# Differential attention with plain fp32 products: key halves on two row tiles, a lagged pipeline over query tiles, and tied engine orders

## The chip, the cores and the metric

One of the eight cores of a Trainium2 chip runs the whole program. The metric is device time in microseconds; a second measurement of the same kernel on the same chip is shown by its median and its extremes. Engines are named as in the profile: PE (matrix products; PEld loads its weights), DVE, ACT, POOL, and SP, which only issues transfers.

## The reference, cut to what matters

The program is a three-branch mixer run for two layers (gated scans, differential attention, a second scan), then a convolution/LRU layer and a mixture of experts. The change touches the attention branch of both layers: 1024 tokens, 4 heads, two score sets (c = 0, 1) of width 64 per head, values of width 128.

```python
q = rope(q, pos) * (DIFF_HD ** -0.5); k = rope(k, pos)      # (2, b, 4, 1024, 64)
s = jnp.einsum('cbhqd,cbhkd->cbhqk', qblk, k)
p = jax.nn.softmax(s, axis=-1)
w = p[0] - lam * p[1]
o = jnp.einsum('bhqk,bhkv->bhqv', w, v)                      # v: (b, 4, 1024, 128)
o = rms_norm(o, norm_w) * (1.0 - lambda_init)
y = merge_heads(o) * silu(g)
```

All of it is float32.

## The kernel before

Most products are made of parts in the type fp32r: an operand x is kept as a rounded half xh (fp32r) and a rest xl = x - xh, and `mm3` (L370 to L374) sums xh·yh, xh·yl and xl·yh in PSUM. In the attention stage the projections of heads 0 and 1 (dq0, dk0, dv0) run first, in the stage of the scans. `rope` (L901 to L924) and `values` (L926 to L932) turn the PSUM results into halves h and lo and store both to DRAM (qd, kd, dvd). Then comes a branch (L616), which all engines pass. Behind it the attention stage begins: head 0 runs while the projections of heads 2 and 3 (dq1, dk1, dv1: 24 steps of 24 matmuls) are mixed in, eight steps per query tile (`Q_PER_TILE`); heads 1 to 3 follow.

A head has eight query tiles of 128 rows. For each tile and each c, `scores` makes pS (128x1024, two PSUM banks) from the query halves, stacked on the 128 rows, against the rounded keys (KH, L989) and their rests (KL, L990): four matmuls of 512 columns. DVE takes the row maximum (L992), ACT the exponential with its row sum (L994). One tile later `combine` forms e0 + e1·sm (L1010), transposes it in eight blocks on PE (pW, L1019), evicts them as halves wTh and wTl (ACT and DVE; one in part by POOL, L1029 to L1031), and for every second tile runs 24 matmuls of 256 columns into pO (`mm3`). For every fourth tile pO is squared, summed over features with ones (pN), normed and written to yd. The two weights of the output projection that are not yet in place, and later the others, are loaded in parts (`wo_load`: 256 KB each), rounded by ACT (L1088), and the rest taken by DVE or POOL (L1089).

From head 1 on, the operands lie in ATh and ATl, the buffers of the normalized input, which are free once the projections have read them. Their loads are issued by POOL, one or two per tile, each behind a POOL instruction (`issue_after`, which ties an instruction's place on its engine behind another's without a semaphore).

A scheduler orders the instructions of each engine from program order, priorities and its own costs; each engine then runs in that fixed order. The pools around the change: pS has 2 buffers, tag "t" of `tp` has 3 (shared by pW, pN and the products of the mixed-in projections), pO has 1.

Of the kernel before, what the change touches and what calls it, by code (L numbers as in the profile page):

```python
# [31 lines left out]
Q_PER_TILE = 8  # L32
PRELOAD = (3, 2, 2)
PER = 2
# [186 lines left out]
def r32(ap):  # L221
    return ap.bitcast(F32)
# [7 lines left out]
def kernel(ctx: ExitStack, tc: tile.TileContext, A: dict, out: bass.AP, upto=99, dbg=None):  # L230
# [42 lines left out]
    qd = dr.tile([4, 2, 64, 2, S], F32, name="qd")  # L273
    kd = dr.tile([4, 2, 64, 2, S], F32, name="kd")
    dvd = dr.tile([4, 128, 2, S], F32, name="dvd")
# [446 lines left out]
    for l in range(DEPTH):  # L722
# [175 lines left out]
        def rope(n, hp, i, w, acc, tr, at, eng=G):  # L898
# [19 lines left out]
            sc = 0.125 if n == 0 else 1.0  # L918
            rope.last = (SC.activation(h, pT, AF.Copy, scale=sc),
                         V.scalar_tensor_tensor(lo, pT, sc, r32(h), op0=OP.mult, op1=OP.subtract))  # L920
            dst = (qd, kd)[n][2 * hp:2 * hp + 2, :, :, :, (i - 1) * 128:(i + 1) * 128]
            for m, t in enumerate((h, lo)):
                for c in range(2):
                    SY.dma_start(dst[:, m, :, c].rearrange("h x t -> x h t"), r32(t)[c * 64:c * 64 + 64])  # L924

        def values(hp, i, w, acc, at):  # L926
            p = tokm(acc[0], w, 256, i, tag=acc[1])
            h, lo = place(at[2], [128, 256], F32R), place(at[3], [128, 256], F32R)
            SC.activation(h, p[:, :256], AF.Copy)
            V.tensor_tensor(lo, p[:, :256], r32(h), op=OP.subtract)  # L930
            for m, t in enumerate((h, lo)):
                SY.dma_start(dvd[2 * hp:2 * hp + 2, :, m, i * 128:i * 128 + 128].rearrange("h p c -> p h c"),  # L932
                             r32(t).rearrange("p (h c) -> p h c", h=2))

        at1 = ((st, "q"), (st, "t2r"), (st, "sgb"), (st, "sgb"))
# [25 lines left out]
        epsm = aw.tile([128, 128], F32, name="epsm", bufs=1)  # L961
        V.memset(epsm, EPS)

        def head_prep(h):

            if h == 0:
                QS, KH, KL, v = (hp_.tile([128, 2, S], F32R, tag=n, name=n) for n in ("QS", "KH", "KL", "v"))
            else:
                a, b = (2, 4) if h == 2 else (6, 0)
                QS, KH, KL, v = ATh[:, a:a + 2], ATl[:, a:a + 2], ATh[:, b:b + 2], ATl[:, b:b + 2]  # L970
            loads = [lambda: G.dma_start(QS, qd[h].rearrange("m x c t -> (m x) c t"))]
            for m, K in enumerate((KH, KL)):
                for d_ in range(2):
                    loads.append(lambda m=m, K=K, d_=d_: G.dma_start(K[d_ * 64:d_ * 64 + 64], kd[h, m]))
            loads.append(lambda: G.dma_start(v, dvd[h]))
            vh, vl = (v[:, m].rearrange("p (k d) -> p k d", k=8) for m in range(2))
            return {"h": h, "ops": (QS, KH, KL, vh, vl), "loads": loads}

        def scores(st, i):

            QS, KH, KL = st["ops"][:3]
            sm = aw.tile([128, 8], F32, tag="sm", name="sm", bufs=3)
            e = []
            for c in range(2):
                p = sc_.tile([128, 2, 512], F32, tag="s", name="pS")
                qq = QS[:, c, i * 128:(i + 1) * 128]
                for kc in range(2):
                    kt = slice(kc * 512, kc * 512 + 512)
                    T.matmul(p[:, kc, :], qq, KH[:, c, kt], start=True, stop=False)  # L989
                    T.matmul(p[:, kc, :], qq, KL[:, c, kt], start=False, stop=True)  # L990
                pf = p.rearrange("p a b -> p (a b)")
                V.tensor_reduce(sm[:, c:c + 1], pf, axis=AX.X, op=OP.max, negate=True)  # L992
                ec = aw.tile([128, S], F32, tag=f"e{c}", name=f"e{c}", bufs=3)
                SC.activation(ec, pf, AF.Exp, bias=sm[:, c:c + 1], accum_out=sm[:, 2 + c:3 + c])  # L994
                e.append(ec)
            return i, e, sm

        def combine(st, i, e, sm):


            qh, qi, qp = i // 4, i % 4, i // 2
            if qi == 0:
                st["dg"] = aw.tile([128, 4, 128], F32, tag="dg", name="dg", bufs=1)
                st["pO"] = op_.tile([128, 512], F32, tag="o", name="pO")
            if i % 2 == 0:
                st["w"] = []
            V.reciprocal(sm[:, 4:5], sm[:, 3:4])
            V.tensor_scalar(st["dg"][:, qi], ident, sm[:, 2:3], sm[:, 2:3], op0=OP.mult, op1=OP.mult)
            V.scalar_tensor_tensor(sm[:, 5:6], sm[:, 4:5], nlam[:, l:l + 1], sm[:, 2:3], op0=OP.mult, op1=OP.mult)
            V.scalar_tensor_tensor(e[0], e[1], sm[:, 5:6], e[0], op0=OP.mult, op1=OP.add)  # L1010
            for g in range(2):
                if i % 2 == 0:
                    st["w"].append((aw.tile([128, 4, 256], F32R, tag="wTh", name="wTh", bufs=2),
                                    aw.tile([128, 4, 256], F32R, tag="wTl", name="wTl", bufs=2)))
                wTh, wTl = st["w"][g]
                p = tp.tile([128, 4, 128], F32, tag="t", name="pW")
                for j in range(4):
                    kt = g * 4 + j
                    T.transpose(p[:, j, :], e[0][:, kt * 128:(kt + 1) * 128], ident)  # L1019
                sl = (slice(None), slice(None), slice((i % 2) * 128, (i % 2) * 128 + 128))  # L1020
                if g == 0:
                    SC.activation(wTh[sl], p, AF.Copy)
                    V.tensor_sub(wTl[sl], p, r32(wTh[sl]))
                elif i % 4 == 3:
                    SC.activation(wTh[sl], p, AF.Copy)
                    V.tensor_sub(wTl[sl], p, r32(wTh[sl]))
                else:
                    wf = aw.tile([128, 4, 128], F32, tag="wf", name="wf")
                    SC.activation(wf, p, AF.Copy)  # L1029
                    G.tensor_tensor(wTh[sl], wf, bc(C("ones")[:, None, :], [128, 4, 128]), op=OP.mult)  # L1030
                    st["pool"] = G.tensor_tensor(wTl[sl], wf, r32(wTh[sl]), op=OP.subtract)  # L1031
            if i % 2 == 0:
                return
            vh, vl = st["ops"][3:]
            cs = slice((qp % 2) * 256, (qp % 2) * 256 + 256)
            for kt in range(8):
                wTh, wTl = st["w"][kt // 4]
                mm3(st["pO"][:, cs], vh[:, kt, :], vl[:, kt, :], wTh[:, kt % 4, :], wTl[:, kt % 4, :], kt == 0, kt == 7)
            if qi < 3:
                return  # L1040
            t = slice(qh * 512, qh * 512 + 512)
            f = 2 + st["h"]
            oT = aw.tile([128, 512], F32, tag="oT", name="oT", bufs=1)
            sq = aw.tile([128, 512], F32, tag="sq", name="sq", bufs=1)
            sg = aw.tile([128, 512], F32, tag="sg", name="sg", bufs=1)
            SY.dma_start(sg, sgd[f][:, t])
            SC.activation(oT, st["pO"], AF.Copy)
            SC.activation(sq, st["pO"], AF.Square, scale=128 ** -0.5)
            p = tp.tile([128, 512], F32, tag="t", name="pN")
            for n in range(4):  # L1050
                c = slice(n * 128, n * 128 + 128)
                T.matmul(p[:, c], C("ones"), sq[:, c], start=True, stop=False)
                T.matmul(p[:, c], epsm, st["dg"][:, n], start=False, stop=True)
            G.tensor_tensor(oT, oT, sg, op=OP.mult)
            SC.activation(sq, p, AF.Ln)
            SC.activation(sq, sq, AF.Exp, scale=-0.5)
            V.tensor_tensor(oT, oT, sq, op=OP.mult)
            SY.dma_start(yd[:, f, t], oT)

        def other_projections():  # L1060
            got = {0: wq1}
            at2 = ((hp_, "st"), (aw, "sg"), (hp_, "sh"), (hp_, "sh"))

            def step(n, i):
# [6 lines left out]
                if i == 2 and n < 2:  # L1071
                    with tc.issue_after(rope.last[0].ins), tc.issue_after(rope.last[1].ins):
                        got[n + 1] = load_w(wp, wsrc(l, ("dq1", "dk1", "dv1")[n + 1]), 8, 256)
# [5 lines left out]
        def wo_load(cc):  # L1079
# [11 lines left out]

            return [lambda i=i: part(i) for i in range(4)]


        def run(n):
            for _ in range(n):
                if steps:
                    steps.pop(0)()
# [975 lines left out]
```

## Time and profile before

| what | value |
|---|---|
| median of 3 runs | 2968.61 us (2963.6 to 2981.33) |
| profiled execution | 2970.06 us, span 2968.2 us, mean granted clock 0.962 |
| attention stage, layer 0 | about 459 to 749 us of the span |
| attention stage, layer 1 | about 1283 to 1564 us |

Every duration below is from the profiled execution, whose own time is 1.5 us above the median. In its rows "busy" is the union of an engine's instructions; matmuls overlap, so the cost of a matmul in a stream is the distance between two starts and not its own duration. The granted clock is a share of TensorE's full 2.4 GHz; 0.5 stands for 1.2 GHz.

### The profile page before, as it was taken

Reading aid. Unit: us, or ns where it says so; the run is one execution under the profiler, and the core shown is the slowest. Engines: PE = TensorE matmul, PEld = TensorE weight load, DVE = VectorE, ACT = ScalarE, POOL = GpSimd, SP = SyncE. Lnnn points to the kernel's source line nnn. Section 1 sums busy time; section 2 is a strip of 40 time slices with the busy share of each in tenths; the row PEclk is TensorE's granted clock in tenths of the full one; section 3 lists DMA queues with packets and bytes.
Section 4 is the critical chain, followed back from the end, with each engine's and each line's share of the span. In section 5 each row is a group of like instructions: output and inputs, shape, how many; then the busy total and the mean of one; then the engine's idle time right before and its main releaser. Section 6 shows DMA issues by size and latency. Waiting matters only on the chain. (4 is left out here: it accounts for less than half of the span.)

```text
span 2968.2 us, 41594 instructions
## 1 busy us (share of the span) xinstructions
PE 2693.9 (91%) x15942; PEld 2252.8 (76%) x15942; DVE 1956.8 (66%) x2806; ACT 1374.3 (46%) x2174; POOL 829.3 (28%) x612
## 2 busy tenths in 40 slices
PE   7999998978999999989789999788799999899968
PEld 6887888867988878888679887588677767566558
DVE  6766565579457676755894592754676776665667
ACT  5343322456443433323664313633576676555545
POOL 1323232345114231313451332610221121211122
PEclk9999999989999999999999999999899999999989
DMA  4122235543422212445434322043797998879852
GB/s 152 61 77 77 86 110 136 132 131 84 138 92 66 80 61 86 120 130 143 132 84 137 108 84 78 29 172 136 302 360 286 356 349 299 318 250 351 331 212 81
DMA packets 158270, 476.25 MB, mean 160 GB/s; under 512 B 16096, under 2 KB 69408, under 8 KB 128736
## 3 DMA queue, kind: packets, MB, share of 16 engines
q1 hardware_dynamic: 144224, 408.07, 39.2%
q0 software_dynamic: 13824, 65.28, 7.5%
q8 instruction: 132, 2.16, 0.3%
q14 instruction: 90, 0.74, 0.1%
HBM read 384.03 MB, written 89.26 MB: 159 GB/s over the span
## 5 line engine op out<-in xcount | busy, mean ns | idle before, releaser
L1602 DVE TENSOR_TENSOR ews<-raw,ews 128x2048 fp32r<-128x2048 f32 x168 | 387.7, 2314 | 176.7 <-ACT ews L1601 175.6
L372 PE MATMUL pK<-wh,ATh 128*128 128x256 f32 x1280 | 374.2, 293 | 30.2 <-DVEq L616 11.4
L1601 ACT ACTIVATE ews<-raw 128x2048 fp32r<-128x2048 f32 x172 | 327.2, 1912 | 114.5 <-PE h L374 73.6
L373 PE MATMUL pK<-wl,ATh 128*128 128x256 f32 x1280 | 371.2, 291 | 7.1 <-DVE wl L355 7.1
L374 PE MATMUL pK<-wh,ATl 128*128 128x256 f32 x1280 | 367.2, 289 | 1.8 <-POOL ATl L1366 1.8
L372 PE MATMUL pF<-ATh,wh 128*128 128x512 f32 (+1 forms) x800 | 320.8, 402 | 1.6 <-ACT g L1287 0.7
L373 PE MATMUL pF<-ATl,wh 128*128 128x512 f32 (+1 forms) x800 | 319.9, 400 | 0.3 <-DVE ATl L343 0.2
L374 PE MATMUL pF<-ATh,wl 128*128 128x512 f32 (+1 forms) x800 | 318.8, 399 | 0.1
L372 PEld LDWEIGHTS pK<-wh,ATh 128*128 128x128 f32 x1280 | 250.2, 196 | 38.3 <-issue 21.4
L373 PEld LDWEIGHTS pK<-wl,ATh 128*128 128x128 f32 x1280 | 250.4, 196 | 14.2 <-DVE wl L355 8.0
L374 PEld LDWEIGHTS pK<-wh,ATl 128*128 128x128 f32 x1280 | 249.0, 195 | 4.2 <-POOL ATl L1366 2.0
L994 ACT ACTIVATE e<-pS,sm 128x1024 f32<-128x1024 f32 x128 | 142.9, 1117 | 108.4 <-DVE sm L992 108.0
L372 PEld LDWEIGHTS pF<-ATh,wh 128*128 128x128 f32 (+1 forms) x800 | 149.6, 187 | 39.6 <-issue 3.7
L373 PEld LDWEIGHTS pF<-ATl,wh 128*128 128x128 f32 (+1 forms) x800 | 149.5, 187 | 38.5 <-issue 5.7
L374 PEld LDWEIGHTS pF<-ATh,wl 128*128 128x128 f32 (+1 forms) x800 | 149.3, 187 | 36.7 <-issue 4.5
L373 PE MATMUL h<-ews,xh 128*128 128x512 f32 (+1 forms) x416 | 165.9, 399 | 8.8 <-DVE ews L1602 8.8
L1802 POOL DMA_INDIRECT xb<-hfd,tab x38 | 60.7, 1598 | 401.8 <-PE pT L1782 389.3
L372 PE MATMUL h<-ews,xh 128*128 128x512 f32 (+1 forms) x416 | 167.1, 404 | 4.4 <-ACT ews L1601 4.4
L374 PE MATMUL h<-ews,xl 128*128 128x512 f32 (+1 forms) x416 | 165.9, 400 | 0.0
L992 DVE TENSOR_REDUCE sm<-pS 128x1 f32<-128x1024 f32 x128 | 154.2, 1213 | 11.7 <-PE pS L990 11.5
L373 PE MATMUL pK<-wo,ATh 128*128 128x256 f32 x512 | 145.8, 285 | 0.0
L374 PE MATMUL pK<-wo,ATl 128*128 128x256 f32 x512 | 145.6, 285 | 0.0
(495 smaller groups left out, 6905.3 us busy)
## 6 DMA issues: line engine op xcount, KB each, us to landing
raw<-in_w_dram SPq DMA_DIRECT2D x192, 1024.0 KB, 9.0
ws<-in_wp_dram SPq DMA_DIRECT2D x64, 512.0 KB, 4.5
xd<-x SPq DMA_DIRECT2D x24, 512.0 KB, 2.6
x<-xd SPq DMA_DIRECT2D x17, 512.0 KB, 4.6
x<-in_x_dram SPq DMA_DIRECT2D x16, 512.0 KB, 6.5
sgd<-sgb SPq DMA_DIRECT2D x32, 256.0 KB, 2.0
sg<-sgd SPq DMA_DIRECT2D x32, 256.0 KB, 3.0
yd<-oT SPq DMA_DIRECT2D x32, 256.0 KB, 2.0
```

The costliest lines, as they stand in the source:

```text
L372: T.matmul(ps, ah, bh, start=first, stop=False)
L373: T.matmul(ps, ah, bl, start=False, stop=False)
L374: T.matmul(ps, al, bh, start=False, stop=last)
L992: V.tensor_reduce(sm[:, c:c + 1], pf, axis=AX.X, op=OP.max, negate=True)
L994: SC.activation(ec, pf, AF.Exp, bias=sm[:, c:c + 1], accum_out=sm[:, 2 + c:3 + c])
L1601: SC.activation(w[:, 0], s_, AF.Copy)
L1602: eng.tensor_tensor(w[:, 1], s_, r32(w[:, 0]), op=OP.subtract)
L1802: G.indirect_dma_start(out=xb[:n], out_offset=None, in_=hfd, in_offset=bass.IndirectOffsetOnAxis(ap=idx, axis=0))
```

## The change

Halves go from attention: q, k and v are stored and loaded once, as fp32 (half the bytes), and all products of the stage are plain fp32 matmuls. The scores of a tile and a c are two matmuls of 512 columns, one on rows 0 to 63 with the first 512 keys and one on rows 64 to 127 with the last 512; the queries are therefore loaded twice, into both row halves. The transposed weights are evicted once, by ACT alone. The value products of a pair of tiles are eight fp32 matmuls in four parts of two. A step `period` of a pipeline emits scores of tile i, the combination of tile i-1, transposes of tile i-2, value parts of tiles i-3 and i-4, squares of i-5 and the norm of i-6; `put` ties each emitted instruction behind the last one on its engine (PE, DVE, ACT). Six empty periods drain it at the end. dg is formed on POOL and holds the epsilon, and the sum pN is one matmul instead of eight. `wo` parts are rounded by DVE and their rest is taken by POOL, one period after their load is issued. The operand loads go to SP's queue, not tied; `Q_PER_TILE` is 5, `PRELOAD` (5, 2, 2), `PER` 3.

```diff
@@ rope / values (halves gone; one store instead of two)
-            h, lo = place(at[2], [128, 2, 256], F32R), place(at[3], [128, 2, 256], F32R)
-            rope.last = (SC.activation(h, pT, AF.Copy, scale=sc),
-                         V.scalar_tensor_tensor(lo, pT, sc, r32(h), op0=OP.mult, op1=OP.subtract))
+            h = place(at[2], [128, 2, 256], F32)
+            rope.last = SC.activation(h, pT, AF.Copy, scale=0.125 if n == 0 else 1.0)
@@ loads
+                a = 2 if h == 2 else 6
+                Q, K, v = r32(ATh[:, a:a + 2]), r32(ATl[:, a]), r32(ATl[:, a + 1])
...
+            for d_ in range(2):
+                rows = slice(d_ * 64, d_ * 64 + 64)
+                loads.append(lambda rows=rows: SY.dma_start(Q[rows], qd[h]))
+                loads.append(lambda rows=rows, d_=d_: SY.dma_start(K[rows], kd[h, :, :, d_ * 512:d_ * 512 + 512]))
+            loads.append(lambda: SY.dma_start(v, dvd[h]))
@@ scores
+            for kc in range(2):
+                rows = slice(kc * 64, kc * 64 + 64)
+                put("pe", lambda: T.matmul(p[:, kc, :], Q[rows, c, i * 128:(i + 1) * 128], K[rows, c, :],
+                                           start=True, stop=True))
@@ turned, weighted
+                put("pe", lambda: T.transpose(p[:, j, :], e[0][:, kt * 128:(kt + 1) * 128], ident))
+            put("act", lambda: SC.activation(w[:, :, (i % 2) * 128:(i % 2) * 128 + 128], p, AF.Copy))
...
+            for kt in (2 * part, 2 * part + 1):
+                put("pe", lambda: T.matmul(pO[:, cs], v[:, kt, :], w[kt // 4][:, kt % 4, :], start=kt == 0,
+                                           stop=kt == 7))
@@ period
+            if b[5] and b[5]["i"] % 4 == 3:
+                squared(b[5])
             for c in range(2):
+                if now:
+                    scores(now, c)
+                if c == 0 and b[1]:
+                    combine(b[1])
+                if b[2]:
+                    turned(b[2], c)
+                for n in (3, 4):
+                    if b[n] and b[n]["i"] % 2 == 1:
+                        weighted(b[n], (n - 3) * 2 + c)
+                if c == 0 and b[6] and b[6]["i"] % 4 == 3:
+                    summed(b[6])
+            if b[6] and b[6]["i"] % 4 == 3:
+                headnorm(b[6])
@@ wo_load: run() calls split one period after the load's issue
-                SC.activation(wh[:, i * 2:i * 2 + 2], s_, AF.Copy)
-                (V if i % 2 else G).tensor_tensor(wl[:, i * 2:i * 2 + 2], s_, r32(wh[:, i * 2:i * 2 + 2]),
-                                                  op=OP.subtract)
+                def split():
+                    put("dve", lambda: V.tensor_copy(wh[:, i * 2:i * 2 + 2], s_))
+                    G.tensor_tensor(wl[:, i * 2:i * 2 + 2], s_, r32(wh[:, i * 2:i * 2 + 2]), op=OP.subtract)
```

How the change moves instructions, at three places. First PE in heads 1 to 3 of layer 0, about two tiles (pS: scores, pW: transposes, pO: value products, pN: the norm's sum). Before:

```order
L989 MATMUL pS<-ATl,ATh 128x512
L990 MATMUL pS<-ATh 128x512
L1019 MATMUL pW<-ident,e_7442 128x128 x8
L372 MATMUL pO<-wTh,ATl 128x256
L1019 MATMUL pW<-ident,e_7485 128x128 x8
L989 MATMUL pS<-ATl,ATh 128x512
L990 MATMUL pS<-ATh 128x512
```

After:

```order
L995 MATMUL pS<-ATl,ATh 128x512 x2
L1027 MATMUL pW<-ident,e_6655 128x128 x4
L1042 MATMUL pO<-wT,ATl 128x256 x2
L1058 MATMUL pN<-sq,cst 128x512
L995 MATMUL pS<-ATl,ATh 128x512 x2
L1027 MATMUL pW<-ident,e_6655 128x128 x4
L1042 MATMUL pO<-wT,ATl 128x256 x2
L995 MATMUL pS<-ATl,ATh 128x512 x2
L1027 MATMUL pW<-ident,e_6701 128x128 x4
L1042 MATMUL pO<-wT,ATl 128x256 x2
```

Before, the order is loose: scores of two tiles lie together, and the 24 value products of a pair come in one run (one of them waits in front of a later transpose here). Now each half of a period is a pair of score matmuls, four transposes and two value products.

Second DVE in the same stretch, with the row maxima (sm<-pS), the combination (e) and the weights (wo). Before:

```order
L992 TENSOR_REDUCE sm<-pS 128x1
L1010 SCALAR_TENSOR_TENSOR e_7005<-e_7013,sm,e_7005 128x1024
L1057 TENSOR_TENSOR oT<-oT,sq 128x512
L992 TENSOR_REDUCE sm<-pS 128x1
L1089 TENSOR_TENSOR wo<-wos,wo 128x512
L1023 TENSOR_TENSOR wTl<-pW,wTh 128x4x128
L1008 TENSOR_SCALAR dg<-ident,sm 128x128
L992 TENSOR_REDUCE sm<-pS 128x1
```

After:

```order
L998 TENSOR_REDUCE sm<-pS 128x1
L1012 RECIPROCAL sm<-sm 128x1
L1013 SCALAR_TENSOR_TENSOR sm<-sm,nlam 128x1
L1015 SCALAR_TENSOR_TENSOR e_6572<-e_6593,sm,e_6572 128x1024
L998 TENSOR_REDUCE sm<-pS 128x1
L1122 CAST wo<-wos 128x512
L998 TENSOR_REDUCE sm<-pS 128x1
```

The rests wTl and dg are gone from DVE; the rounding of a part of wo (CAST) stands once per period between two row maxima, in 16 of the 32 periods of a layer.

Third the operand loads of heads 1 and 2, before on POOL between its other work, now on SP. After:

```order
L927 DMA dvd<-pl 128x2x128 x7
L976 DMA ATl<-kd 64x2x512
L975 DMA ATh<-qd 64x2048 x3
L927 DMA dvd<-pl 128x2x128
L976 DMA ATl<-kd 64x2x512
L975 DMA ATh<-qd 64x2048
L976 DMA ATl<-kd 64x2x512
L977 DMA ATl<-dvd 128x1024
L976 DMA ATl<-kd 64x2x512
L977 DMA ATl<-dvd 128x1024
```

The ten loads of both heads stand together, around the last store of the mixed-in projections; of the first four, three are head 2's (1.25 MB), before most of head 1's 2 MB.

## Rows read from the trace of the kernel before

**Rows 1.** Windows: length; busy us (count) by engine; clock, DMA share, GB/s.

```profile
459.00:558.00 99.00, 94.40 (x704) 90.54 (x705) 52.58 (x94) 26.27 (x46) 22.75 (x34) 0.96 0.48 123
558.00:749.00 191.00, 153.04 (x903) 129.19 (x902) 163.35 (x219) 118.47 (x216) 99.86 (x77) 0.91 0.45 120
...
1380.00:1564.50 184.50, 151.78 (x911) 128.06 (x910) 162.99 (x219) 118.00 (x216) 99.81 (x77) 0.93 0.46 124
460.00:480.00 20.00, 16.30 (x104) 15.38 (x103) 7.35 (x17) 2.74 (x4) 3.47 (x6) 0.84 0.99 253
680.00:720.00 40.00, 36.50 (x236) 30.64 (x235) 38.54 (x54) 27.33 (x50) 19.37 (x14) 1.00 0.35 91
735.00:740.00 5.00, 2.10 (x16) 1.87 (x17) 4.96 (x8) 4.13 (x8) 4.47 (x4) 1.00 0.13 49
...
745.00:750.00 5.00, 3.15 (x16) 2.93 (x16) 4.76 (x7) 2.18 (x4) 2.65 (x2) 0.75 0.40 114
```

**Rows 2.** Windows of L994 alone: length, ACT busy us (two records each), clock, DMA.

```profile
558.00:749.00 191.00, 65.01 (x108) 0.91 0.45 120
680.00:720.00 40.00, 16.87 (x28) 1.00 0.35 91
```

**Rows 3.** PE groups, 558 to 749 us: busy, mean ns | idle before, releaser.

```profile
L989 PE MATMUL pS<-ATl,ATh 128*128 128x512 f32 x96 | 42.4, 441 | 19.3 <-ACT e L994 19.3
...
L1019 PE MATMUL pW<-ident,e 128*128 128x128 f32 x232 | 32.7, 283 | 5.8 <-DVE e L1010 5.0 <-ACT wf L1029 0.3
...
L373 PE MATMUL pO<-wTl,ATl 128*128 128x256 f32 x91 | 28.4, 313 | 7.8 <-DVE wTl L1023 7.8
```

**Rows 4.** DVE groups, 558 to 749 us.

```profile
L992 DVE TENSOR_REDUCE sm<-pS 128x1 f32<-128x1024 f32 x53 | 63.9, 1212 | 4.0 <-PE pS L990 3.9
L1010 DVE SCALAR_TENSOR_TENSOR e<-e,sm,e 128x1024 f32<-128x1024 f32 x27 | 36.2, 1341 | 0.6
L1023 DVE TENSOR_TENSOR wTl<-pW,wTh 128x512 fp32r<-128x512 f32 x30 | 20.3, 681 | 0.8 <-ACT wTh L1022 0.8
...
L1089 DVE TENSOR_TENSOR wo<-wos,wo 128x512 fp32r<-128x512 f32 x8 | 6.2, 775 | 11.5 <-ACT wo L1088 11.5
```

**Rows 5.** ACT groups, 558 to 749 us.

```profile
L994 ACT ACTIVATE e<-pS,sm 128x1024 f32<-128x1024 f32 x54 | 60.2, 1117 | 35.5 <-DVE sm L992 35.4
...
L1088 ACT ACTIVATE wo<-wos 128x512 fp32r<-128x512 f32 x16 | 9.8, 634 | 21.3 <-DMA wos<-in_wo_dram 21.3
```

**Rows 6.** PE in order of time (start, us): scores and transposes in a stream.

```profile
688.72 0.39 PE L990 MATMUL pS<-ATh 128*128 128x512 f32 x1
688.95 1.04 PE L1019 MATMUL pW<-ident,e 128*128 128x128 f32 x8
```

**Rows 7.** PE in order of time: one fp32 product of 512 columns.

```profile
154.00 1.02 PE L580 MATMUL pN<-sq,cst 128*128 128x512 f32 x2
...
155.09 0.40 PE L372 MATMUL pF<-ATh,wh 128*128 128x512 f32 x1
```

**Rows 8.** PE in order of time: fp32 products on two row tiles (scan stage).

```profile
304.65 0.61 PE L531 MATMUL pU<-gvv,ki 128*128 128x128 f32 x4
305.19 0.37 PE L542 MATMUL pf<-Qd,Kd 32*128 32x128 f32 x1
305.20 0.37 PE L542 MATMUL pb<-Qd,Kd 32*128 32x128 f32 x1
305.40 0.27 PE L542 MATMUL pf<-Qd,Kd 32*128 32x128 f32 x1
...
306.08 0.27 PE L542 MATMUL pb<-Qd,Kd 32*128 32x128 f32 x1
...
306.62 0.40 PE L372 MATMUL pF<-ATh,wh 128*128 128x512 f32 x1
```

**Rows 9.** PE groups, 459 to 558 us, those with waits.

```profile
L372 PE MATMUL pK<-wh,ATh 128*128 128x256 f32 x192 | 56.8, 296 | 5.9 <-DVEq L616 5.9
...
L990 PE MATMUL pS<-KL,QS 128*128 128x512 f32 x24 | 10.1, 430 | 2.7 <-DMA KL<-kd 2.7
```

More of the change, by code (lines that the diff above doesn't have):

```diff
@@ L968, in head_prep @@
             else:
[L969 to L983, printed above, removed]
-            for c in range(2):
[L985 to L1058, printed above, removed]
@@ new lines, in turned @@
+        def turned(q, g):
+            st, i, e = q["st"], q["i"], q["e"]
+            if i % 2 == 0:
+                st["w"] = st.get("w", [])[:2 * g] if g else []
+                st["w"].append(aw.tile([128, 4, 256], F32, tag="wT", name="wT", bufs=4))
+            p = tp.tile([128, 4, 128], F32, tag="t", name="pW")
+            for j in range(4):
+                kt = g * 4 + j
+                put("pe", lambda: T.transpose(p[:, j, :], e[0][:, kt * 128:(kt + 1) * 128], ident))
+            w = st["w"][g]
+            put("act", lambda: SC.activation(w[:, :, (i % 2) * 128:(i % 2) * 128 + 128], p, AF.Copy))
+            q["w"] = st["w"]
@@ new lines, in weighted @@
+        def weighted(q, part):
+            st, qp = q["st"], q["i"] // 2
+            if part == 0:
+                if qp % 2 == 0:
+                    st["pO"] = op_.tile([128, 512], F32, tag="o", name="pO")
+                q["pO"] = st["pO"]
+            pO, v, w = q["pO"], st["ops"][2], q["w"]
+            cs = slice((qp % 2) * 256, (qp % 2) * 256 + 256)
+            for kt in (2 * part, 2 * part + 1):
+                put("pe", lambda: T.matmul(pO[:, cs], v[:, kt, :], w[kt // 4][:, kt % 4, :], start=kt == 0,
+                                           stop=kt == 7))
@@ new lines, in summed, with headnorm @@
+        def summed(q):
+            p = q["pN"] = tp.tile([128, 512], F32, tag="t", name="pN")
+            put("pe", lambda: T.matmul(p, C("ones"), q["sq"], start=True, stop=True))
+        def headnorm(q):
+            sq, oT, qh = q["sq"], q["oT"], q["i"] // 4
+            put("act",
+                lambda: SC.activation(sq, q["pN"], AF.Ln),
+                lambda: SC.activation(sq, sq, AF.Exp, scale=-0.5))
+            G.tensor_tensor(oT, oT, sq, op=OP.mult)
+            SY.dma_start(yd[:, 2 + q["st"]["h"], qh * 512:qh * 512 + 512], oT)
@@ new lines, in period, with back @@
+        def period(now, qs):
+            def back(n):
+                return qs[-1 - n] if len(qs) > n else None
+            qs.append(now)
+            b = [back(n) for n in range(7)]
+            if b[5] and b[5]["i"] % 4 == 3:
+                squared(b[5])
+            for c in range(2):
+                if now:
[11 more added lines that the diff above has]
+                headnorm(b[6])
@@ L1107 @@
         proj = other_projections()
-        late = None
+        qs = []
         for h in range(4):
@@ L1115 @@
             for i in range(8):
-                now = (ops[h],) + scores(ops[h], i)
-                if late:
-                    combine(*late)
-                late = now
+                period({"st": ops[h], "i": i, "e": [],
+                        "sm": aw.tile([128, 8], F32, tag="sm", name="sm", bufs=4)}, qs)
                 if h < 3 and i == PRELOAD[h]:
@@ L1122 @@
                 for load in next_loads(h):
-                    with tc.issue_after(ops[h]["pool"].ins):
-                        load()
+                    load()
                 run(per)
-        combine(*late)
+        tail = turn["act"]
+        for _ in range(6):
+            period(None, qs)
+            run(0)
         p2.close()
```

90 lines of the change are left out of this document (67 added, 23 removed).

## The prediction

> **What bounds the kernel now.** I first cut the span into stages with the windows view, since the shares of the whole span mix stages with different limits. The attention stage of layer 0 has two stretches [rows 1]. In 459 to 558 us the projections of heads 2 and 3 run mixed with five tiles of head 0, and PE is busy 94.4 of 99.0 us: PE bounds it. From 558 to 749 us 27 tiles are left (108 records of L994, two records for each of two exponentials per tile [rows 2]) and PE is busy 153 of 191 us at a mean granted clock of 0.91, so PE doesn't bound this stretch. DVE does, with interruptions: in 680 to 720 us DVE is busy 38.5 of 40 us, and the 28 records of L994 there are 7 tiles, 5.71 us each. At that rate 27 tiles would take 154 us; the other 37 of the 191 us are stalls and the end.
>
> The groups by line then name the waits. PE's largest is 19.3 us in front of a score matmul until an exponential has freed its PSUM buffer; 7.8 us go to the rest wTl, 5.0 to the combination [rows 3]. The exponentials in turn wait 35.4 us for the row maxima, so the ring goes back to DVE. And ACT stands 21.3 us in front of the rounding of a weight part (L1088) until its load has landed [rows 5]; DVE stands 11.5 us for ACT behind that [rows 4]. These are the stalls: a load that is late stops an engine that the scores need. Layer 1 has the same stretch from 1380 to 1564.5 us, 184.5 us [rows 1].
>
> So the question is what the stretch costs when DVE has less to do, the tied order takes the late loads out of the way, and PE pays for fp32.
>
> **The price of an fp32 product.** The sum pN of the scans is an fp32 matmul of 512 columns in a dense stream: it starts at 154.00, the second matmul behind it at 155.09, and one fp32r matmul of 512 columns (0.23, from the distance in [rows 6]) lies between. So it takes 0.86 us, in two records of 0.43 [rows 7]; 256 columns take 0.43, 128 columns 0.107 per record. A transpose takes 0.11: eight span 1.04 us, of which the last's modelled duration is 0.27 [rows 6].
>
> **Scores.** Removed per tile and c: four fp32r matmuls, 4 x 0.23 = 0.93 us. Added: two fp32 matmuls of 512 columns with 64 rows each. No row shows these. Bounds: side by side 0.86, one after the other 1.72. The nearest rows are fp32 products on two row tiles in the scans [rows 8]: pf and pb start 0.01 us apart, again and again, sixteen records (305.19 to 306.08) in eight steps of 0.11. They run side by side from the first record on. But the excursion has a price: the four records of L531 that start at 304.65 are done at 305.08 (4 x 0.107); the second matmul behind it starts at 306.62, so the stream is back at 306.39. That is 1.31 us for 8 x 0.107 = 0.86 us of work: 0.45 us for going into the row tiles and out. I take 0.86 + 0.44 = 1.30 us for a pair, with 0.86 and 2.16 as ends: every half period enters and leaves the row tiles, since transposes of all 128 rows follow.
>
> **Values, transposes, norm.** A pair of tiles takes eight fp32 matmuls of 256 columns, 3.44 us, where 24 fp32r ones took about 24 x 0.12 = 2.9. Transposes stay. pN is one matmul of 0.86 us for four tiles in place of eight of 128 columns (two records each, 1.7 us).
>
> **PE's work in the long stretch.** With the counts of before: 26 tiles' scores (96 records of L989 for heads 1 to 3 are 24 tiles [rows 3], and two of head 0's are left), 52 x 1.30 = 67.6; 232 transposes, 25.1; 15 pairs of values, 51.6; 7 norms, 6.0. Sum 150.3 us, that is 2.60 + 0.86 + 1.72 + 0.22 = 5.40 per tile.
>
> **Is PE the bound then?** DVE per tile: two maxima 2.42, the combination 1.34, a quarter of a product of 128x512 (0.68, as L1023) 0.17, together 3.9 and the small ones; the rests wTl and dg are gone. In the 16 periods with a weight part 0.78 more, 4.7 [rows 4]. ACT: two exponentials of 1.12 and less than 2 us for the rest. Both are under 5.40. The ring also closes in time: a score pair (1.3), its maximum (1.2) and exponential (1.1) are some 4 us with the handovers, and a buffer comes back after one period. So PE should be the bound, at 0.96 or more of the full clock, as it is at 1.00 in 680 to 720 us, where it is busy 91%.
>
> **What PE's work doesn't cover**, 11 us per layer: the end, where the last maximum, exponential, combination, transposes and eviction follow one another (before, PE idled 4.8 us of 735 to 740 and 745 to 750 [rows 1]; I keep 5); head 1's operands, 2; DVE's short lead in the periods with a weight part and the seams of heads, 4. Of head 1: in SP's order 2.75 MB lie up to its last key part, and at 253 GB/s, the rate of 460 to 480 us [rows 1], that is 11 us and a few for landing. The work ahead of its first scores is six half periods, about 16 us: barely hidden. If it weren't, head 1 would wait, and not SP alone; behind those loads only weight parts queue, each a period ahead of its use. POOL loses the evictions and gets dg and all the rests of the weights; nothing on PE waits for these within a period.
>
> So the stretch takes 150.3 + 11 = 161 us: 30 less in layer 0, 23.5 less in layer 1.
>
> **The first stretch.** PE bounds it and its work grows: 12 pairs of scores by 0.37, a pair of values by 0.6, together 5 us. Against that stand the halved bytes: the 2.7 us wait for KL [rows 9] goes with that operand, some 1 us for KH too, and SP, which PE waits for at the branch for 5.9 us, has half the stores to issue; I take 1.5 for that. Net 0 in both layers. Spreading the projections over more tiles (five steps each) moves work, it adds none.
>
> **Sum.** 2970.06 - 53.5 = 2916.6 us for an execution like the profiled one; the median of before is 1.5 us below that, which gives **2915 us**.
>
> **The rivals.**
> 1. *DVE stays the bound*, because the tied order makes it wait its turn: 5.71 per tile instead of 5.40. For it: the weight parts bring DVE to 4.7 and more, and POOL works beside it. Against: 3.9 in the other half of the tiles. 26 x 0.31 = 8 us per layer: 2932.
> 2. *The weight parts stall DVE as they stalled ACT.* The rounding now stands between two maxima, and an unlanded part stops both. For: ACT lost 21.3 us so. Against: each part has a period between issue and use. If all of it returns, 2 x 21.3: 2958.
> 3. *The row tiles overlap by half.* If matmuls start and end strictly in program order and the second's first record can't start before the first's last, a pair takes three records: 0.43 more for 128 pairs, 55 us: 2970. Against it: [rows 8], where pb's first record starts with pf's first. The Trainium skill's page "TensorE: Matmul & The Clock Gate" (Part 3, under "What overlaps and what doesn't") says that matmuls are strictly in order in start and end, without reordering; by a literal reading of that the sum would be this rival's 2970. The rows of this case differ from that reading at 128 columns; none shows 512.
> 4. *Slower: the row tiles don't overlap at 512 columns*, because the two streams share something that short ones don't fill. A pair then costs 2.16 us: 0.86 x 128 = 110 us more, 3025. This decides from 0.42 more per pair (53.5 / 128) for no gain; from 0.65 more the kernel is over 1% slower. For it only that no row has such a length.
>
> That the change doesn't do what it says is excluded by the order of the instructions: pairs of scores stand side by side in each half period.
>
> **How the numbers follow.** Forecast 0.70, rivals 0.12, 0.06, 0.05, 0.07. A measurement here can tell about 1%, 29.7 us, from no change. Faster by that: the forecast and most of rival 1, 0.80. Within: the rest of it, rivals 2 and 3, 0.13. Slower: rival 4, 0.07. The range reaches down to a price of 1.08 for a pair (half of the 0.44 hidden, 28 us less) with 3 instead of 11 us uncovered, 2915 - 28 - 16 = 2871, and up to rival 2: 2870 to 2960; rivals 3 and 4 are left out.
>
> **What the profile after would show.** Right: in the long stretch PE is busy over 92%, a period of 5.3 to 5.6 us, the first records of a score pair starting within 0.02 us of each other, the wait of scores for exponentials under 5 us per layer, ACT no longer waiting for weights. Wrong: a period of 5.7 with DVE over 95% (rival 1); waits of the rounding on DVE for its load (rival 2); a pair of 1.7 (rival 3) or 2.2 us (rival 4). A long wait of a head's first scores for their loads would make the 2 us too small; a lower granted clock in the stretch would raise every term of PE.

## The result, and the profile after

The changed kernel takes **2928.4 us** in the median of four runs (2926.4 to 2938.8), the kernel before 2966.1 us beside it; the ratio is 0.9871 with a 95% interval of 0.9828 to 0.9914. So it is 38 us faster where 53.5 were forecast; 2928 lies inside the range of 2870 to 2960.

The stretches of the stage in the profiled execution after (its own time is 2938.8 us, the slowest of the four; columns as in [rows 1], the engines in the order PE, PEld, DVE, ACT, POOL). The first four lines are the two stretches of each layer, the fifth four periods in the middle, then the first 20 us behind the branch in both layers, then the end:

```profile
454.60:555.00 100.40, 96.65 (x681) 84.00 (x682) 39.97 (x71) 27.27 (x47) 16.34 (x30) 0.94 0.28 71
555.00:729.30 174.30, 159.08 (x750) 90.86 (x748) 121.92 (x166) 108.98 (x196) 61.06 (x57) 0.99 0.37 101
1259.10:1360.00 100.90, 96.47 (x677) 83.73 (x678) 39.98 (x71) 27.48 (x47) 16.13 (x30) 0.93 0.28 70
1360.00:1538.00 178.00, 160.36 (x754) 90.87 (x753) 122.33 (x167) 109.17 (x197) 60.99 (x57) 0.98 0.36 99
617.98:640.69 22.71, 21.21 (x98) 11.36 (x98) 17.75 (x26) 15.04 (x27) 11.11 (x11) 1.00 0.55 145
454.60:475.00 20.40, 17.47 (x80) 13.75 (x81) 4.99 (x11) 2.30 (x4) 0.45 (x1) 0.69 0.45 105
1259.10:1280.00 20.90, 17.29 (x73) 13.02 (x74) 5.17 (x11) 2.41 (x4) 0.45 (x1) 0.67 0.44 103
705.85:735.00 29.15, 22.20 (x118) 18.88 (x117) 11.55 (x18) 14.07 (x25) 5.10 (x4) 0.88 0.39 118
```

In the long stretch PE went from 80% busy at a clock of 0.91 to 91% at 0.99, and DVE from 86% to 70%: the bound has moved to PE. But four periods take 22.71 us, 5.68 per tile and not 5.40, and PE works only 21.21 of them. The groups of PE in 555 to 729 us say why (columns as in [rows 3]):

```profile
L995 PE MATMUL pS<-ATl,ATh 64*128 64x512 f32 x192 | 54.6, 641 | 0.0
L1042 PE MATMUL pO<-wT,ATl 128*128 128x256 f32 x192 | 50.7, 390 | 7.5 <-DVE oT L1052 7.5
L1042 PE MATMUL pO<-wT,v 128*128 128x256 f32 x56 | 14.5, 382 | 1.0 <-DVE oT L1052 1.0
L1058 PE MATMUL pN<-sq,cst 128*128 128x512 f32 x16 | 8.3, 599 | 1.7 <-POOL sq L1054 1.7
L372 PE MATMUL pK<-wo,ATh 128*128 128x256 f32 x12 | 4.0, 331 | 2.5 <-ACT ATh L1188 2.5
```

The scores' 19.3 us of waiting for exponentials [rows 3] are gone, and ACT no longer waits for weight parts. What is new is a wait of the value products for oT, the product of pO with the gate. One such wait in order of time, all engines:

```profile
637.16 0.38 PE L1042 MATMUL pO<-wT,ATl 128*128 128x256 f32 x1
637.47 1.13 PE L995 MATMUL pS<-ATl,ATh 64*128 64x512 f32 x4
637.74 1.11 ACT L1000 ACTIVATE e<-pS,sm 128x1024 f32<-128x1024 f32 x1 [1.08 <-DVE sm L998]
638.53 0.66 PE L1027 MATMUL pW<-ident,e 128*128 128x128 f32 x4
638.84 0.59 ACT L1029 ACTIVATE wT<-pW 128x512 f32<-128x512 f32 x1
639.32 0.60 ACT L1051 ACTIVATE sq<-pO 128x512 f32<-128x512 f32 x1
639.95 0.69 DVE L1052 TENSOR_TENSOR oT<-pO,sg 128x512 f32<-128x512 f32 x1 [1.91 <-ACT sq L1051]
640.69 0.48 PE L1042 MATMUL pO<-wT,ATl 128*128 128x256 f32 x1 [1.50 <-DVE oT L1052]
```

The last value product of a group starts at 637.16. Its square could follow at 637.5, but ACT's tied order has an exponential and an eviction ahead of it, so it starts at 639.32; DVE's product follows only then, and the single pO buffer is free at 640.7. PE, whose tied order lets nothing else go first, stands 1.50 us in every fourth period.

Where the time went, from starts of the same events in both traces (us from PE's first matmul behind the branch; "last maximum" is the start of the last L992 or L998):

| | layer 0 before | after | layer 1 before | after |
|---|---|---|---|---|
| to the last mixed-in projection | 97.0 | 100.7 | 95.7 | 101.6 |
| from there to the last maximum | 179.8 | 149.3 | 173.7 | 151.3 |
| from there to the end of the output projection | 114.5 | 119.9 | 113.5 | 121.1 |

The long stretch up to the last maximum gained 30.5 and 22.4 us. The first stretch gave back 3.7 and 5.9, the end 5.4 and 7.6. Together that is 30.3 us of the 31.2 by which the two profiled executions differ.

The gain of the long stretch is not a faster tile. In the kernel before, behind the last weight part (its rounding starts at 640.7 us in layer 0), four tiles take 22.5 us, and DVE is busy 21.76 of them:

```profile
694.71:717.20 22.49, 20.23 (x129) 16.85 (x128) 21.76 (x32) 15.41 (x28) 10.94 (x7) 1.00 0.08 24
```

That is 5.6 us per tile, no more than the 5.68 after. What went are the stalls among the weight parts: by the starts of the row maxima, the eight tiles of head 1 took 8.0 us each in layer 0 and 7.7 in layer 1 before, 5.7 and 5.9 after. In layer 0 that is 19 us, beside the 21.3 us that ACT stood for weight parts [rows 5].

### The profile page after: what moved, and what is told of

It reads as the page before. It is cut to its first block, busy times and chain, and to the rows that moved or that the text cites. A ratio compares the mean times of both kernels' runs of the same rounds, so it can differ in the third digit from the quotient of the medians.

```text
span 2936.7 us, 39989 instructions
## 1 busy us (share of the span) xinstructions
PE 2705.7 (92%) x15462; PEld 2156.6 (73%) x15462; DVE 1832.6 (62%) x2614; ACT 1351.8 (46%) x2126; POOL 740.5 (25%) x564
## 5 line engine op out<-in xcount | busy, mean ns | idle before, releaser
L373 PE MATMUL pK<-wl,ATh 128*128 128x256 f32 x1280 | 371.9, 291 | 7.3 <-DVE wl L355 7.3
L998 DVE TENSOR_REDUCE sm<-pS 128x1 f32<-128x1024 f32 x128 | 156.2, 1221 | 112.2 <-PE pS L995 112.2
L372 PE MATMUL pK<-wo,ATh 128*128 128x256 f32 x512 | 148.6, 290 | 10.5 <-ACT ATh L1188 10.5
L373 PE MATMUL pK<-wo,ATh 128*128 128x256 f32 x512 | 147.0, 287 | 0.0
```

Of the source, the lines that this page charges most:

```text
L372: T.matmul(ps, ah, bh, start=first, stop=False)
L373: T.matmul(ps, ah, bl, start=False, stop=False)
L998: put("dve", lambda: V.tensor_reduce(sm[:, c:c + 1], pf, axis=AX.X, op=OP.max, negate=True))
```

## The experiments

Each is an edit of the changed kernel. All ratios are to the kernel before, run on the same chip; its medians on the three chips used are 2966.1, 2969.9 and 2969.5 us. A "stage" is the time from PE's first matmul behind the branch to the end of the output projection, from the traces.

**The base once more.**

> The changed kernel once more, as the base for the runs beside it. Its profiled execution took 2938.8 us against a median of 2928.4: if the 10 us are chance, the median here is again 2926 to 2932 and a new profile shows the same periods (22.72 us per four query tiles); if the profile slows the program, the profiled time is again about 10 us above the others.

2929.6 us, 0.9867 (0.9847 to 0.9888); its profiled execution took 2931.9 us, with the same 22.7 us per four periods. So the 10 us of the first profile did not come again. Of the 7.2 us between the two profiled spans 6.8 lie outside the attention stages, and what they were is open: that rest of the program takes from 2177 to 2197 us in the thirteen profiles of this case, whatever the edit.

**Are the row tiles really side by side?**

```diff
-                rows = slice(kc * 64, kc * 64 + 64)
+                rows = slice(0, 64)
                 put("pe", lambda: T.matmul(p[:, kc, :], Q[rows, ...], K[rows, c, :], ...
```

> Both score products of a pair go through rows 0 to 63 (the second repeats the first 512 keys, so half of the scores are those of other keys); everything else stays. If the two products of a pair overlap in full on two row tiles (my theory), a pair that takes 1.15 us now takes four records of 0.43 one after the other, 1.72 and about 0.1 for going in: 0.65 more for each of 128 pairs, some 80 us: 3000 to 3015 us, slower than the kernel before. If they overlap by half (rival 3 of the prediction), a pair grows by 0.43, 55 us: 2985. If they don't overlap now, nothing changes: 2928. If DVE were the bound and PE had slack (rival 1), less than half of the 80 us would come out.

3021.9 us in its one execution, 7 us above the expected range. PE in order of time, first in the changed kernel, then with one row tile (start, us, and "x4" for four records in a row):

```profile
655.17 1.13 PE L995 MATMUL pS<-ATl,ATh 64*128 64x512 f32 x4
656.23 0.66 PE L1027 MATMUL pW<-ident,e 128*128 128x128 f32 x4
```

```profile
645.04 1.98 PE L995 MATMUL pS<-ATl,ATh 64*128 64x512 f32 x4
646.96 0.65 PE L1027 MATMUL pW<-ident,e 128*128 128x128 f32 x4
```

From the scores' start to the transposes' it is 1.06 us on two row tiles and 1.92 on one: 0.86 apart, two records of 0.43. The overlap is full at 512 columns, so rivals 3 and 4 fall. (The time grows by 92 us and not by 0.86 for each of 128 pairs, 110 us, since PE's wait for pO shrinks from 1.50 to 0.31 us per group of four tiles.) The Trainium skill's "TensorE: Matmul & The Clock Gate" (Part 3, "What overlaps and what doesn't") says that matmuls are strictly in order in start and end; taken record by record, that would have made it rival 3's three records. This trace shows two. On one row tile the steps between the records are 0.53, 0.43 and 0.43, and 0.52 to the transposes: the first step, and the way out, carry 0.1 us each.

**Projection steps emitted first.**

```diff
             for i in range(8):
+                if h == 0:
+                    run(per)
                 period({"st": ops[h], "i": i, ...
...
-                run(per)
+                if h:
+                    run(per)
```

> While head 0 runs, the five projection steps of a tile are emitted ahead of the tile's period and not behind it, so that PE has 20 us of work that needs no load when the stage begins. Theory: the first stretch became 3.7 and 5.9 us longer because PE waits 2.9 and 3.6 us for head 0's key part right after the 5 us at the branch, and runs on at 1.2 GHz until about 471 us; with work in between both go: 3 to 7 us less per layer, 2914 to 2922 us. Rival: the half clock comes from the branch alone and the work of tile 0 is only moved behind the projections, where it costs a period of its own (5.7 us): 2928 to 2935.

2929.7 us, 0.9871 (0.9848 to 0.9894): no change, as the rival had it (the first stretch is some 6 us shorter, the long one 5 longer), but not the test that it was meant to be. The first scores still came 9.7 us behind the branch on PE and waited for their keys (4.3 us in two pieces in layer 0): the scheduler, not the order of emission, had put them there.

**Value sums in two halves.**

```diff
-            if b[5] and b[5]["i"] % 4 == 3:
-                squared(b[5])
+            for n, m in ((6, 1), (5, 3)):      # per pair, on 256 columns
+                if b[n] and b[n]["i"] % 4 == m:
+                    squared(b[n])
...
+                q["pO"] = st["pO"] = both[0][:, (qp % 2) * 256:(qp % 2) * 256 + 256]   # one buffer for good
```

> Squares and the product with the gate are taken per pair of tiles, on 256 columns, and the next pair writes the other half of the PSUM buffer. Theory: in the long stretch PE waits 1.50 us in every fourth period until ACT's square and DVE's product have freed the only buffer for value sums; without that wait the four periods take 21.0 to 21.2 us instead of 22.72, five of them per layer and the end: 8 to 9 us less per layer, 2910 to 2913 us. Rival: the tied order of DVE and ACT sets the period as much as PE (rival 1 of the prediction): the extra pieces on ACT (0.35 us) and DVE (0.4 us) take what the wait gives back, four periods stay at 22.3 or more, 2922 to 2930 us. If reads of one half still hold back writes of the other, nothing changes.

2932.9 us, 0.9886 (0.9860 to 0.9913). The wait did not go, it came twice as often: PE stands 1.05 to 1.15 us twice in four periods, which take 23.7 us in place of 22.7:

```profile
609.00:632.70 23.70, 21.56 (x100) 11.47 (x100) 17.86 (x27) 15.46 (x31) 10.99 (x11) 1.00 0.52 133
```

The half that PE wants to write is not the one that is read; the program's order holds back the whole bank. In the changed kernel DVE's read of pO also starts only when ACT's read has ended (0.03 us behind, in seven of eight groups of each layer). The Trainium skill's "PSUM — Partial Sum Buffer" ("PSUM bank collisions raise a hardware error") says that two engines must not touch the same partitions of one bank at once, reads included, and that access is to be ordered by bank and not by address; this program's waits agree: smaller pieces of one bank buy nothing. What the chip would do without them no run here shows.

**The square first.**

```diff
                 for n in (3, 4): ... weighted(b[n], (n - 3) * 2 + c)
+                if hold:          # c == 1 and b[4]["i"] % 4 == 3
+                    squared(b[4])
+                    put("act", *held)       # this half's exponential and eviction
+                    held.clear()
```

> In the half period that ends a group of four tiles, ACT's square and DVE's product with the gate stand right behind the last value products, ahead of the exponential and the eviction of that half; nothing else moves. Theory: the 1.50 us (with its restart 1.75) that PE waits in every fourth period is ACT's order: the square stands behind an exponential and an eviction that take until 1.9 us after the sums are ready. With the square first, the square and the product end before PE needs the buffer: four periods take 21.0 to 21.3 us, 16 to 19 us less in both layers: 2910 to 2914 us. Rival: the exponential that now comes 0.6 us later holds back the next scores (two PSUM buffers): the wait moves to the scores and four periods stay above 22 us: 2925 to 2932 us.

**2903.9 us**, 0.9773 (0.9755 to 0.9792). Four periods:

```profile
600.70:621.74 21.04, 21.04 (x101) 11.36 (x100) 18.25 (x27) 14.94 (x28) 11.02 (x10) 1.00 0.49 123
```

The wait is gone and PE is busy without a gap, 5.26 us per tile. DVE is busy 18.25 of 21.04: it never was the bound, though 5.68 had looked like rival 1's 5.71. The time is 6 us under the expected range: the stages of this run take 358.6 and 355.2 us, 15 less than the base in the mean; some 10 of them lie in the long stretch, some 4 in the end.

**A shorter drain.**

```diff
-                if c == 0 and b[6] and b[6]["i"] % 4 == 3:
+                if now and c == 0 and b[6] and b[6]["i"] % 4 == 3:
                     summed(b[6])
+                if not now and c == 1 and b[5] and b[5]["i"] % 4 == 3:
+                    summed(b[5])
+                    headnorm(b[5])
-            if b[6] and b[6]["i"] % 4 == 3:
+            if now and b[6] and b[6]["i"] % 4 == 3:
                 headnorm(b[6])
```

> In the empty periods at the end, sum and norm of a group follow its squares in the same period, not in the next. Theory: the end of the stage became 5.4 and 7.6 us longer because the output projection's rows 0 to 3 need head 3's first group, whose norm now comes with a lag of six periods: PE waits 2.5 us, then 2.6 us behind the store and the reload of that group, and runs at 1.2 GHz after it. With the norm a period earlier the second wait goes or shrinks: 4 to 8 us less per layer, 2914 to 2922 us. Rival: the end is bound by the chain of the last tile (maximum, exponential, combination, transposes, values), whatever the norm does: 2927 to 2932 us.

2927.4 us, 0.9849 (0.9824 to 0.9875): unclear in the times: its interval takes in the base, and the median lies in the rival's range. In the traces the stages take 367.7 and 370.6 us; four stages of the base took 369.9 to 374.0, 371.9 in the mean. That is 2.7 us per layer, less than expected; the end alone is 3.7 shorter (116.1 and 118.0 us). The chain in the changed kernel, SP's waits and then PE:

```profile
SPq L1066 <- POOL oT L1065: 13.6, 3, 8.8
```

```profile
725.65 0.91 SPq L1186 DMA_DIRECT2D ym<-yd  x2
728.64 1.33 ACT L1188 ACTIVATE ATh<-ym 128x512 fp32r<-128x512 f32 x2 [4.41 <-DMA ym<-yd]
729.32 0.39 PE L372 MATMUL pK<-wo,ATh 128*128 128x256 f32 x1 [2.58 <-ACT ATh L1188]
```

The output projection needs head 3's first group, which comes out of the pipeline six periods late; its reload can only follow its store, and SP stands 8.8 us at that store for POOL. In layer 0 that store is issued 19.0 us behind the start of the last maximum, in this run 15; in the kernel before it was 2.6.

**The first scores tied behind three projection steps.**

```diff
             for i in range(8):
+                if h == 0 and i == 0:
+                    run(3)
+                    turn["pe"] = mm3.last     # the last matmul of a projection
                 period({"st": ops[h], "i": i, ...
```

> The first score product of head 0 is tied behind three steps of the projections on PE, so that it can't stand in PE's order while its operands load (the emission order alone left it where it was). Theory: the wait for the first keys (2.9, 3.6, 4.3 and 2.5 us in the four stages profiled so far) goes, and with it the fall back to 1.2 GHz that follows it until some 16 us behind the branch (about 3 us): 5 to 7 us less per layer, 2915 to 2920 us. Rival: the half clock belongs to the idle branch alone and only the wait goes: 2 to 4 us per layer, 2922 to 2926 us; or what tile 0 loses by its later start comes back at the end of the stretch: no change.

2921.0 us, 0.9824 (0.9796 to 0.9852), 1 us above the expected range. That is 9 us under the base in the medians, with intervals that just overlap; in the traces the stages take 366.8 and 367.9 us, 4.5 under the base. PE still waits 1.6 to 1.8 us for the keys: three steps are too few. The clock of the first 20 us is 0.75, where the base had 0.69 and 0.67.

**Weights rounded by ACT, at once.**

```diff
-                    put("dve", lambda: V.tensor_copy(wh[...], s_))
+                    put("act", lambda: SC.activation(wh[...], s_, AF.Copy))
...
-                splits.append(split)
+                split()
```

> The weight parts are rounded by ACT, as in the kernel before, and in the order right behind the issue of their load, not a period later on DVE; the rest of the pipeline stays. If it is the period between load and use that took away the stall (ACT lost 21.3 us to it in layer 0), each of the 16 parts per layer stops ACT again for the 2 to 3 us of a landing, and the scores behind it: half or more comes back, 10 to 25 us per layer, 2950 to 2980 us. Rival: the lagged pipeline absorbs a late part by itself, since ACT has over a microsecond to spare in each period: 2928 to 2935 us.

2954.2 us, 0.9944 (0.9925 to 0.9963): 23 to 25 us come back, the low end of what was expected, but not for the reason given. No rounding waits for a landing; ACT's groups in 575 to 700 us, then a part of one wait in order of time:

```profile
L1122 ACT ACTIVATE wo<-wos 128x512 fp32r<-128x512 f32 x16 | 10.0, 624 | 0.0
```

```profile
594.26 1.11 ACT L1000 ACTIVATE e<-pS,sm 128x1024 f32<-128x1024 f32 x1 [2.13 <-DVE sm L998]
595.85 0.63 ACT L1122 ACTIVATE wo<-wos 128x512 fp32r<-128x512 f32 x1
596.36 0.59 ACT L1051 ACTIVATE sq<-pO 128x512 f32<-128x512 f32 x1
597.74 1.30 PE L1042 MATMUL pO<-wT,ATl 128*128 128x256 f32 x3 [3.07 <-DVE oT L1052]
```

ACT's rounding (0.63 us) stands ahead of the square, and the exponential ahead of both is about 1 us late as well, so PE's wait grows from 1.50 to 3.07 us (in four of the five groups from 590 to 700 us), and that has a second price. Windows around this wait:

```profile
590.00:594.70 4.70, 4.67 (x23) 2.20 (x21) 4.16 (x5) 2.54 (x5) 2.77 (x2) 1.00 0.39 112
594.70:597.80 3.10, 0.06 (x1) 0.06 (x1) 0.81 (x2) 2.26 (x5) 1.25 (x2) 1.00 0.01 3
597.80:601.00 3.20, 3.20 (x8) 1.33 (x8) 2.58 (x4) 1.69 (x3) 1.79 (x3) 0.55 0.53 164
```

After 3.1 us of idleness PE is granted 0.55 for the next 3.2 us, near 1.2 GHz; after the 1.50 us of the changed kernel it kept 1.00.

**Scores of a tile together.**

```diff
-                if now:
-                    scores(now, c)
+                if now and c == 0:
+                    scores(now, 0)
+                    scores(now, 1)
```

> Both score pairs of a tile are issued one behind the other at the start of a period (c = 0, then c = 1), the combination and everything else behind them; squares stay where the change has them. Theory: full overlap of two row tiles costs nothing per record, but going into row tiles and out costs some 0.3 us (in the run with one row tile the first record's step is 0.533 and the last's 0.520 where the inner ones are 0.429, and 0.09 lies ahead): once per period instead of twice saves 0.3 us per period. And the value products then come 1.1 us later behind a group's end, so that most of the 1.50 us wait for the PSUM buffer of value sums goes. Four periods 19.9 to 20.5 us instead of 22.72, and 2 us of the first stretch per layer: 2888 to 2900 us. Rival: the scores of the next tile need both PSUM buffers at once, behind maximum, maximum, combination and two exponentials in a row: they wait, and four periods take 21.5 us or more: 2905 to 2930 us.

**2895.1 us**, 0.9755 (0.9731 to 0.9779). Four periods take 19.93 us without a gap on PE, a period without pN 4.67 in place of 5.02:

```profile
602.80:622.73 19.93, 19.93 (x100) 11.95 (x98) 17.92 (x26) 14.91 (x28) 10.49 (x11) 1.00 0.65 159
```

```profile
610.87 1.99 PE L995 MATMUL pS<-ATl,ATh 64*128 64x512 f32 x8
612.79 0.66 PE L1027 MATMUL pW<-ident,e 128*128 128x128 f32 x4
```

Eight records take 1.92 us to the transposes where twice four took 2.12; the rest of the 0.35 lies ahead of the scores and in the first transpose. That is the price of one trip into row tiles and back. The Trainium skill's "TensorEngine Tiling (Array Packing)" (Key Properties) says that a change of tiling mode drains TensorE; the trace agrees in that such a change costs time, and gives the price here, 0.35 us. One wait is new: head 1's first scores stand 1.4 and 2.8 us for their keys, which the prediction had called barely hidden.

**The three edits that paid, together** (scores together, four steps ahead of the first score, the shorter drain).

> Scores of a tile together, the first scores of head 0 tied behind four projection steps, and in the empty periods the norm in the period of its squares. If the gains add: the run with scores together, less 4 to 5 us per layer for the first stretch (as the run with three steps showed for wait and clock together) and 2 to 4 us per layer for the end: 12 to 18 us under that run, about 2875 to 2885 us if it gives 2890. Rival: the end is bound by the last tile's own chain and the first stretch by the load, and one of the two gives nothing: 5 to 9 us under that run.

**2873.2 us**, 0.9678 (0.9663 to 0.9693), the fastest version: 22 us under the one before, more than expected, both layers alike (341.1 and 341.4 us per stage). With four steps the wait for the first keys is gone in both layers:

```profile
459.50:480.00 20.50, 20.46 (x139) 18.36 (x140) 10.16 (x23) 4.90 (x7) 0.45 (x1) 0.92 0.65 168
1233.90:1254.40 20.50, 20.49 (x138) 18.25 (x138) 9.95 (x22) 4.74 (x7) 0.45 (x1) 0.90 0.65 169
```

The gain lies ahead of the last maximum, where the stages are 11.4 and 17.7 us shorter than in the run with scores together (head 1's wait for its keys is gone as well). From the last maximum to the end of the output projection it still takes 119.1 us, 0.2 and 1.8 less: the shorter drain gave next to nothing here, and the end is not solved.

**No ties.**

```diff
-                with tc.issue_after(turn[eng].ins) if eng in turn else nullcontext():
-                    turn[eng] = f()
+                turn[eng] = f()
```

> The changed kernel without the ties between the instructions that a period emits: the scheduler orders PE, DVE and ACT by its own costs. Theory: most of the 30 us that the long stretch gained in layer 0 comes from less work on DVE and the lag between the steps, and the ties only hold the order; untied, scores run ahead and the order gets loose as before: waits of scores for exponentials come back, a tile takes 5.7 to 6.0 us and the time is 2930 to 2950 us. Rival: the ties are what makes the gain, and without them the stalls at weight parts and PSUM buffers return: 2955 us or more. Other rival: the ties cost the wait for the value sums' buffer, and the scheduler places the square better: 2905 to 2920 us.

2958.6 us, 0.9960 (0.9940 to 0.9981). PE's and DVE's groups in 560 to 720 us (the lines stand one lower):

```profile
L994 PE MATMUL pS<-ATl,ATh 64*128 64x512 f32 x183 | 54.8, 676 | 17.1 <-ACT e L999 17.0
L1041 PE MATMUL pO<-wT,ATl 128*128 128x256 f32 x160 | 38.7, 390 | 0.2 <-DVE oT L1051 0.2
```

```profile
L1121 DVE CAST wo<-wos 128x512 fp32r<-128x512 f32 x16 | 7.5, 475 | 11.3 <-DMA wos<-in_wo_dram 11.2
```

The waits of before are back: 17.0 us for exponentials, 11.2 for weight parts, now on DVE. They lie where the weight parts come in: the untied order rounds the 16 parts of a layer within 49 us, the changed kernel one per period over 108, and head 1's tiles take 6.8 us each in place of 5.7 and 5.9. Behind the parts four tiles of layer 0 take 22.30 us without ties, less than the 22.71 with them; the wait for pO is nearly gone there:

```profile
684.00:706.30 22.30, 20.68 (x101) 12.07 (x100) 16.50 (x23) 15.02 (x27) 4.49 (x6) 1.00 0.06 24
```

The end takes 112.5 and 113.9 us untied, as in the kernel before: the longer end belongs to the tied order and not to the lag alone. In all, some 28 of the 38 us that the change gains hang on the ties. What ties alone would have given the kernel before was not run.

## Why the prediction was right in its range and 13 us off in its value

- *PE becomes the bound*: right once the wait for pO is taken away, when PE is busy every moment (21.04 of 21.04). As it was made, the kernel missed two of the signs that the prediction had named: PE is busy 91% and not over 92%, and a period takes 5.68 and not 5.3 to 5.6 us.
- *Scores 1.30 us a pair*: the full overlap was right, the price of the trip too high. In the stream a pair costs 0.09 ahead, 1.06, and 0.05 in the first transpose, 1.20. Values (0.43 each) and transposes were right. With a quarter of pN (0.22) and of a restart of 0.1 us the tile is 5.26 us, not 5.40.
- *"The ring also closes in time ... So PE should be the bound"*: the step that failed. I followed the ring of pS alone. pO is a ring of one, and in the tied order its release stands on ACT behind an exponential and an eviction. It cost 1.67 us per four tiles (22.71 against 21.04), and the period came out at 5.68. The sum of the long stretch was still met up to the last maximum, 30.5 and 22.4 us gained for 30 and 23.5, and that was luck: the wait, 0.42 us for each of 26 tiles or 11 us, was offset by a tile's work too dear by 0.14 (4 us) and by the 6 us set aside beside the end. The shares were off too: the prediction counted 5.71 us per undisturbed tile before, where the starts of the maxima give 5.6, so that the tile gained nothing and the stalls all of it.
- *The end, 5 us*: mis-sized. It gave back 5.4 and 7.6 us beyond what the end before had cost. In the tied order a pipeline with six periods of lag brings the norm of head 3's first group out late, its store 19.0 us behind the last maximum instead of 2.6 (layer 0).
- *The first stretch, net 0*: 3.7 and 5.9 us dearer. I credited 2.7 us for the wait for KL, "which goes with that operand", and some 1 us for KH. The waits for keys were 3.7 us in both layers and are 2.9 and 3.6, now all for KH, because the first scores stand 10 us behind the branch, sooner than before (12.1 and 13.9); and behind the wait the clock fell (0.69 and 0.67 in the first 20 us; before, 0.84 in 460 to 480 us, [rows 1]).
- *Weight parts*: right that they no longer stall, but the lag between load and use is not what removes it. Rounded at once by ACT they still don't wait for a landing in the tied order, which spaces them by a period; without ties they come closer together and do wait, on DVE.
- *Rivals*: 1 had nearly the measured period for the wrong engine; 2 did not come (no wait of the rounding); 3 and 4 are excluded by the run with one row tile.

The two mis-sized terms, end and first stretch, are 22.6 us in the two profiles, where the forecast of 53.5 is 22.3 above the 31.2 by which the two executions differ. In the medians it is 16 us above the 37.7 measured. An exact closure of that is not to be had: the stages of the changed kernel differ by up to 3.6 us from one execution to the next, and the rest of the program by more.

## What to carry to other kernels

When an order is tied by hand, follow every buffer of one, not only the ring in view: what frees it may stand behind work of the next tile on another engine. In such an order a lag of n periods is paid at the end too, by whatever needs the last groups. Compare a tile where nothing disturbs it before calling it faster: here the change removed stalls, and only the later edits, the square first and the scores together, made the tile itself shorter. And if a number agrees with a rival, look at who is idle before believing its mechanism.

## What the runs showed of the hardware that I had not expected

- Two fp32 products of 64 rows and 512 columns on two row tiles take the time of one, two records of 0.43 us; one trip into row tiles and back costs 0.35 us in this stream.
- A stop of PE of 1.50 us left the granted clock at 1.00, one of 3.1 us was followed by 3.2 us at 0.55; by an estimate from these clocks (3.2 x 0.45), the longer stop cost 1.4 us of PE's work beside its own length.
